# First attention: eight chunks a head made into rounded parts on GpSimd, values stored in class layout, maxima a chunk later, ada sums a step later

## Chip, cores and metric

One core of a Trainium2 chip. The metric is the device time in microseconds (us) of one execution. The kernel before takes 3302.08 us, the median of three runs (3301.21 to 3302.14).

## What is computed

Two transformer blocks on one sequence of 2048 tokens, width 1024, in f32. The change lies in the first block: its dilated attention, and two helpers of it. Shortened, for each of 12 heads of 64 dimensions:

```python
for window, dilation in ((128, 1), (512, 4), (2048, 16)):
    o_i, lse_i = dilated_window_attn(q, k, v, window, dilation)
mix_w = softmax(stack(lses))
o = sum(mix_w * outs)
attn_out = o * silu(g_attn)
```

The second block starts from `mod = silu(c) @ w_ada + b_ada`, a vector of 6144 numbers. The kernel makes it during the first block's projections.

## The kernel before, in words

**Stages.** `phase_a` makes the projections of the first block (0 to 754 us of the trace): first the values for 16 token tiles, then queries and keys with their rotation, then the gates and the convolution. `phase_b` is the first attention (754 to 1160 us). After it come the output projection, the second block and its experts. The order of the instructions is written out by hand under `tc.manual_schedule()`; each engine runs its own instructions in that order, and semaphores make it wait for the others. SP's queue issues nearly all DMAs, also in order. GpSimd (POOL) issues one DMA a head.

**Values.** `v_store` (L400) stores the values of token tile `t` to the scratch tensor `s_v`. A value row has 128 columns: 64 of a rounded high part and 64 of the rest. `load_v` (L756) loads one head's values as they lie (`v1`, 128 rows of 8 KB, one DMA); `turn_v` (L762) then makes the second arrangement `v2`, in which the rows go by class (token modulo 4 in groups of 32), by 16 GpSimd copies of 32x512 (L765).

**The head loop of `phase_b`.** `for h in range(H1)` runs over 12 heads. A loop has 20 chunks (`k`). In the loop of head `h`, PE computes the products of head `h` and the scores of head `h + 1`. A chunk does, in this order:

- `tpose` (L856): up to four 128x128 blocks of the exponentials are transposed by TensorE into a PSUM tile `pt` (three buffers);
- scores of the next head (`score`, L797, two matmuls; L798, a DVE operation that adds the mask and takes the minimum), 33 calls spread over chunks 0 to 13;
- exponentials (`expo`, L829, on ACT), one chunk ahead (`LA = 1`);
- `parts` (L859): the transposed chunk is copied from PSUM to SBUF. As *H*, ACT casts it to a rounded high part (L188) and DVE subtracts to get the rest (L189). As *A* or *V*, it is copied whole, in f32, by ACT or DVE (L865);
- `products(2)`: matmuls with the values (`mms`, L876) of the chunk two chunks back. A chunk in two parts takes two matmuls a piece; a whole chunk takes one f32 matmul, which the trace shows as two instructions.

In heads 0 to 10 the chunks go `HAHHAHHHHHAHVHVVHHVA`; head 11 has an order of its own. At the end of a group, `after1` copies a PSUM bank into `T` (one of four on DVE, three on ACT), and `after2` (L896, DVE) adds the classes.

**Maxima and sums.** The minima of the (negated) scores of the next head are joined over the arrangements by 16 small matmuls (`joint`, L818) at chunk 14 and by DVE (`joint2`, L824) at chunk 15; then the next head's first exponentials start. The sums of the exponentials of a head are rearranged by `total` (16 small GpSimd copies, L839) when the last exponential is issued. In chunk 2 of the next loop `total2` adds (L845), takes the reciprocal (L846), transposes on PE (L848), copies (L850) and stores. In chunk 6, `rest` issues GpSimd's DMA (L905), which adds half of `T` to `s_t` in DRAM after SP's store of `T`.

**Keys and queries.** `load_qk` loads head `h + 2` from SP's queue. GpSimd doubles the two keys (`repeat`, L661, 64x2048 each, chunks 7 and 8) and orders the query (`order`, L777, four of 128x512, chunks 10 to 13). The ordered query `q2` has two buffers. In head 10 GpSimd also makes the low halves of four tiles of `w_out` (`WO.split`, L681), in chunks 8, 9, 16 and 17.

**Ada.** `ada_step` runs once (three times twice) beside each of 34 projections in `phase_a`. A step ends the pair made before (`end`: two matmuls on PE, L290, then DVE adds and a store), rounds the next pair (`finish`: ACT, then DVE), sums one more block on DVE (L268, L270) and loads another.

The numbers of the profile's lines are those of this code:

Of the kernel before, what the change touches and what calls it, by code (L numbers as in the profile page):

```python
# [18 lines left out]
NT = 16  # L19
# [74 lines left out]
def prep(inp):  # L94
# [35 lines left out]
    "s_v": ([H1, 128, NT, 128], F32),  # L130
# [167 lines left out]
def phase_a(tc, A, K):  # L298
    nc = tc.nc
    ident, eps = K["ident"], K["eps"]  # L300
    with ExitStack() as es:
# [23 lines left out]
        with ExitStack() as e1:  # L325
# [74 lines left out]
            def v_store(t, vs):  # L400
                nc.sync.dma_start(A["s_v"][:, :, t].rearrange("h p d -> p h d"), vs.rearrange("p h a d -> p h (a d)").bitcast(F32))
# [184 lines left out]
        with tc.manual_schedule():  # L586
            last = None
            loads, sums = [], []
            na = 0

            def ada_step(more):
                nonlocal na
                ada.end()
                if sums:
                    ada.finish(*sums.pop(0))
                if len(loads) > 1 or loads and not more:
                    sums.append(ada.sums(*loads.pop(0)))
                if more and na < 32:
                    loads.append((na, ada.load(na)))
                    na += 1  # L600

            for _ in range(2):
                ada_step(True)
            bias = Bias(tc, A, ea)
            for i, j in enumerate(order):
                nxt = order[i + 1] if i + 1 < len(order) else None
                if i == 9:
                    while sums or loads or ada.late:
                        ada_step(na < 32)
                    ea.close()  # L610
                    K["qk"] = QK(tc, A, K)
                    K["qk"].load(0)
                for n in range(4):
                    p = proj(j, n)
                    if last:
                        done(*last)
                    last = j, n, p
                    if i < 9 and i * 4 + n > 1:
                        for _ in range(1 + (i in (2, 4, 6) and n == 0)):
                            ada_step(na < 32)  # L620
                        if i == n == 1:
                            bias.heads(ps)
                    if n == 1 and nxt and nxt not in W:
                        wsplit(nxt)
                        more = [x for x in order[i + 2:] if x not in W and x not in RAW]
                        if more:
                            wload(more[0])
            done(*last)


class QK:
# [10 lines left out]
    def open(self):  # L642
        self.add(1)
        with self.tc.using_default_side("right"):
            self.q2p = self.es.enter_context(self.tc.tile_pool(name="q2B", bufs=2, reuse_waits="tile"))
# [12 lines left out]
    def repeat(self, h, n, eng):  # L658

        t = self.T[h][n]  # L660
        eng.tensor_copy(t[64:], t[:64].bitcast(F32))  # L661
# [64 lines left out]
def phase_b(tc, A, K):  # L726
# [5 lines left out]
    with ExitStack() as es:  # L732
# [18 lines left out]
        m2 = cp.tile([128, 512], F32, name="m2")  # L751
        HD = {}
# [3 lines left out]
        def load_v(h):  # L756
            v1, v2 = (vv[h % 2].tile([128, KC, 256], F32R, name=n).rearrange("p a b -> p (a b)") for n in ("ph", "pl"))
            v1, v2 = v1.rearrange("p (t d) -> p t d", d=128), v2.rearrange("p (c a d) -> p c a d", c=4, d=128)
            nc.sync.dma_start(v1.bitcast(F32), A["s_v"][h])
            HD.setdefault(h, {}).update(v1=v1, v2=v2)  # L760

        def turn_v(h, i):  # L762

            d, (c, u) = HD[h], divmod(i, 4)
            nc.gpsimd.tensor_copy(d["v2"][QD[u], c], d["v1"][QD[c], u::4].bitcast(F32))  # L765
# [44 lines left out]
        WHOLE = [{k: {"A": nc.scalar.copy, "V": nc.vector.tensor_copy}[e] for k, e in enumerate(w) if e != "H"} for w in ("HAHHAHHHHHAHVHVVHHVA", "VVHAVHVVHHVHHHHHHHHH")]  # L810
# [20 lines left out]
        def total(h):  # L831
            d = HD[h]
            L = d["den"]
            E = st.tile([128, 4, 4], F32, name="E2", bufs=2)
            Lr = L.rearrange("p (g c a) -> p g c a", g=2, c=4)
            copy = (nc.gpsimd if h < H1 - 1 else nc.vector).tensor_copy
            for c in range(4):
                for u in range(4):
                    copy(E[QD[c], u, :], Lr[QD[u], 1, c, :])  # L839
            d["E2"] = E  # L840

        def total2(h):
            L, E = HD[h]["den"], HD[h]["E2"]
            r = st.tile([128, 16], F32, name="r", bufs=2)
            nc.vector.tensor_add(r.rearrange("p (a u) -> p u a", u=4), L[:, :16].rearrange("p (u a) -> p u a", u=4), E)  # L845
            nc.vector.reciprocal(r, r)  # L846
            p = ps_t.tile([128, 512], F32, name="pt")
            nc.tensor.transpose(p[:16, :128], r, ident)  # L848
            rt = st.tile([16, 128], F32, name="rt", bufs=1)
            nc.vector.tensor_copy(rt, p[:16, :128])  # L850
            nc.sync.dma_start(A["s_r"][h].rearrange("(t p) -> t p", p=128), rt)
# [7 lines left out]
        def parts(p, w, k, h):  # L859

            hi = pp.tile([128, 512], F32R, name="ph")
            W = WHOLE[h == H1 - 1]
            if k in W:
                whole = hi.bitcast(F32)
                W[k](whole[:, :w], p[:, :w])  # L865
                return whole,
            lo = pp.tile([128, 512], F32R, name="pl")
            split(nc, hi[:, :w], lo[:, :w], p[:, :w])
# [10 lines left out]
        def chunks(h, last_T):  # L879
# [11 lines left out]
            def after1(a):  # L891
                (nc.vector.tensor_copy if a == 1 else nc.scalar.copy)(T[:, a * 512:(a + 1) * 512], O.pop(a))
# [17 lines left out]
            V1, V2 = d["v1"], d["v2"]  # L910
            for a in range(4):
# [4 lines left out]
                            lambda pt, a=a, t0=t0: mms(bank(a), pt, [(V1[:, t0, :], 0, 0, 256), (V1[:, t0 + 1, :], 256, 128, 256)], True, False), None))  # L916
                bl = [on(t0 + 2), off(t0 + 3), on(t0 + 3)] + ([off(t0)] if a else [])
                td = [(V1[:, t0 + 2, :], 0, 256, 256), (V1[:, t0 + 3, :], 256, 384, 128)] + ([(V1[:, t0 - 1, :], 384, 0, 128)] if a else [])
# [20 lines left out]
        with tc.manual_schedule():  # L939
# [17 lines left out]
            for i in range(16):  # L957
                turn_v(0, i)
# [13 lines left out]
            LA, SC, JD = 1, 14, 1  # L972
            TV = {k: (2 * i, 2 * i + 1) for i, k in enumerate((4, 5, 9, 14, 15, 16, 17, 18))}
            L10, W10, W11 = (4, 13), (8, 9, 16, 17), (4, 6, 8, 10)
            wo_tile = lambda i: (QKs.q2p if i % 4 == 3 else QKs.P[i // 4]).tile([128, S], F32R, name=("q", "ka", "kb", "q2")[i % 4])
# [5 lines left out]
            for h in range(H1):  # L981
# [23 lines left out]
                for k, (_, bl, mm, aft) in enumerate(ch):  # L1005
                    if more and k == SC + JD:
# [8 lines left out]
                    while ne < min(need, 32):  # L1015
                        EX[ne]()
                        ne += 1
                        if ne == 32:
# [6 lines left out]
                    products(2)  # L1025
                    if k == SC and more:
                        joint(h + 1)
                    if k == 2 and h:
                        total2(h - 1)
                    if k == 6 and h:  # L1030
                        HD[h - 1].pop("rest")()
                    if h + 2 < H1:
                        if k in (7, 8):
                            QKs.repeat(h + 2, ("ka", "kb")[k - 7], nc.gpsimd)
                        if 10 <= k < 14:
                            order(h + 2, k - 10, nc.gpsimd)
                    if more:
                        for i in TV.get(k, ()):
                            turn_v(h + 1, i)
# [10 lines left out]
                    if not more:  # L1050
# [9 lines left out]
                        if k == 16:  # L1060
                            total2(h)
                            for e in range(2):
# [1506 lines left out]
```

## Time and profile before

| what | value |
|---|---|
| median of three runs | 3302.08 us |
| profiled execution, its own time | 3293.63 us |
| its span, first to last instruction | 3291.8 us |
| first attention in the span | 754 to 1160 us |
| one head of it, from one joint to the next (859.68 to 890.31) | 30.63 us |

The trace is of one execution. PE is TensorE's matmuls, PEld its weight loads, DVE VectorE, ACT ScalarE, POOL GpSimd. The time of a stretch is that of the engine that has no idle time in it; an engine with idle time can take more work as long as nobody waits for its result. Where a row gives start times, the time of a step on a busy engine is read from one start to the next, since a matmul's end is modelled and instructions overlap.

### The profile page before, as it was taken

The numbers are of one execution on the slowest core, as the hardware profiler recorded it, in microseconds if no ns is written. First come the engines' busy times: TensorE is split into PE (matmuls) and PEld (weight loads), VectorE is DVE, ScalarE is ACT, GpSimd is POOL, SyncE is SP. The second block draws the span as 40 slices with busy tenths as digits, with TensorE's granted clock in tenths as the row PEclk, the third lists the DMA queues.
The fourth block names the chain that finished last, engine by engine and source line by source line (L and its number), as shares of the span: only waits on it lengthen the run. The fifth ranks groups of instructions, "written<-read, shape, count | busy, mean of one in ns | idle before, by whom it ended". The sixth has DMA issues, their size and how long they took to land. (4 is left out here: it accounts for less than half of the span.)

```text
span 3291.8 us, 49939 instructions
## 1 busy us (share of the span) xinstructions
PE 3110.4 (94%) x19200; PEld 2766.1 (84%) x19200; DVE 2021.7 (61%) x4077; ACT 1437.4 (44%) x3072; POOL 675.4 (21%) x784
## 2 busy tenths in 40 slices
PE   9999999999999889789998999489999999999998
PEld 8988877888888767689986778389999999999997
DVE  5445557627888835547777476755565665565654
ACT  4322211105888723436657332244444444454443
POOL 0022210005566447311121010100110010010010
PEclk9999999999999999899999999789999999999999
DMA  5433357405555478544444765346666556665653
GB/s 167 138 132 122 117 184 233 142 20 143 148 126 142 117 218 232 140 132 154 146 139 153 235 187 175 129 180 212 211 211 213 205 205 212 211 217 206 208 203 102
DMA packets 200885, 556.83 MB, mean 169 GB/s; under 512 B 26512, under 2 KB 119580, under 8 KB 180294
## 3 DMA queue, kind: packets, MB, share of 16 engines
q1 hardware_dynamic: 186902, 499.73, 45.3%
q0 software_dynamic: 13456, 53.37, 7.0%
q8 instruction: 151, 2.47, 0.3%
q14 instruction: 88, 0.72, 0.1%
q10 hardware_dynamic: 288, 0.53, 0.0%
HBM read 425.29 MB, written 130.37 MB: 169 GB/s over the span
## 5 line engine op out<-in xcount | busy, mean ns | idle before, releaser
L2481 PE MATMUL mm<-xh,wh 128*128 128x256 f32 x2048 | 581.9, 284 | 0.2 <-ACT xh L188 0.2
L2481 PE MATMUL mm<-xl,wh 128*128 128x256 f32 x2048 | 580.7, 284 | 0.1
L2481 PE MATMUL mm<-xh,wl 128*128 128x256 f32 x2048 | 580.5, 283 | 0.0
L2475 DVE TENSOR_TENSOR wl<-raw,wh 128x1024 fp32r<-128x1024 f32 x380 | 453.8, 1222 | 177.0 <-ACT wh L2474 177.0
L2481 PEld LDWEIGHTS mm<-xh,wh 128*128 128x128 f32 x2048 | 394.2, 192 | 1.1 <-ACT xh L188 0.4
L2481 PEld LDWEIGHTS mm<-xl,wh 128*128 128x128 f32 x2048 | 394.1, 192 | 1.0 <-DVE xl L189 0.4
L2481 PEld LDWEIGHTS mm<-xh,wl 128*128 128x128 f32 x2048 | 394.1, 192 | 0.0
L2474 ACT CAST wh<-raw 128x1024 fp32r<-128x1024 f32 x384 | 390.1, 1049 | 0.0
L481 PE MATMUL mm<-hH,wl 128*128 128x512 f32 x832 | 325.2, 391 | 1.9 <-DVE wl L189 1.9
L481 PE MATMUL mm<-hH,wh 128*128 128x512 f32 x832 | 325.6, 391 | 0.0
L481 PE MATMUL mm<-hL,wh 128*128 128x512 f32 x832 | 325.4, 391 | 0.0
L2536 POOL DMA_INDIRECT out_dram<-yo,idx x32 | 63.1, 1973 | 750.7 <-DVE yo L2535 583.0
L829 ACT ACTIVATE s<-s,nm 128x256 f32<-128x256 f32 (+3 forms) x384 | 202.1, 531 | 19.5 <-DVE nm L824 19.5
L189 DVE TENSOR_TENSOR pl<-pt,ph 128x512 fp32r<-128x512 f32 (+1 forms) x269 | 176.6, 662 | 48.7 <-ACT ph L188 46.6
L2531 PE MATMUL y<-wh,hh 128*128 128x512 f32 x512 | 204.4, 399 | 0.0
L2531 PE MATMUL y<-wh,hl 128*128 128x512 f32 x512 | 200.1, 391 | 0.0
L2531 PE MATMUL y<-wl,hh 128*128 128x512 f32 x512 | 199.7, 390 | 0.0
L188 ACT CAST ph<-pt 128x512 fp32r<-128x512 f32 (+1 forms) x269 | 149.8, 562 | 110.4 <-PE pt L856 40.9
L481 PEld LDWEIGHTS mm<-hH,wl 128*128 128x128 f32 x832 | 157.2, 189 | 35.2 <-DVE wl L189 2.3
L481 PEld LDWEIGHTS mm<-hH,wh 128*128 128x128 f32 x832 | 157.1, 189 | 35.2 <-issue 1.7
L481 PEld LDWEIGHTS mm<-hL,wh 128*128 128x128 f32 x832 | 157.0, 189 | 32.2
L798 DVE CUSTOM_DVE_ANT_0 s<-ps,m 128x256 f32<-128x256 f32 (+3 forms) x384 | 156.9, 449 | 35.2 <-PE ps L797 33.8
(474 smaller groups left out, 6938.1 us busy)
## 6 DMA issues: line engine op xcount, KB each, us to landing
raw<-in_wg SPq DMA_DIRECT2D x32, 2048.0 KB
raw<-in_wd SPq DMA_DIRECT2D x32, 2048.0 KB
raw<-in_wu SPq DMA_DIRECT2D x31, 2048.0 KB
adaw<-in_wada SPq DMA_DIRECT2D x32, 768.0 KB
x<-in_x SPq DMA_DIRECT2D x32, 512.0 KB
wraw<-in_w1t SPq DMA_DIRECT2D x26, 512.0 KB
s_v<-vs SPq DMA_DIRECT2D x16, 768.0 KB
q<-s_q SPq DMA_DIRECT2D x12, 1024.0 KB
```

The costliest lines, as they stand in the source:

```text
L188: nc.scalar.copy(hi, src)
L189: (e or nc.vector).tensor_tensor(lo, src, hi.bitcast(F32), op=ALU.subtract)
L481: nc.tensor.matmul(p, a[:, k, :], b[:, k, tk], start=i == 0, stop=i == 3 * KC - 1)
L798: nc.vector.tensor_tensor_reduce(sv, p[:, :w], mask[:, mask.shape[1] - w:], 1.0, TOP, ALU.add, ALU.min, d["nm"][:, i:i + 1])
L829: nc.scalar.activation(sv, sv, AF.Exp, bias=d["nm"][:, i:i + 1], scale=-1.0, accum_out=d["den"][:, i:i + 1])
L2474: nc.scalar.copy(hi[:, c], RAW[i][:, c])
L2475: eng.tensor_tensor(lo[:, c], RAW[i][:, c], hi[:, c].bitcast(F32), op=ALU.subtract)
L2481: nc.tensor.matmul(p, a.rearrange("p (k f) -> p k f", k=KC)[:, k, w0:w0 + 128], b[:, k, :], start=i == 0, stop=i == 3 * KC - 1)
L2531: nc.tensor.matmul(ys[sl][:, cs], a[:, kk, sl * 128:sl * 128 + 128], b[:, k, cs], start=kk == 0 and j == 0, stop=kk == 7 and j == 2)
L2536: nc.gpsimd.indirect_dma_start(out=A["out"], out_offset=bass.IndirectOffsetOnAxis(ap=idx[:, sl:sl + 1], axis=0), in_=y, in_offset=None, co ...
```

## The change

- `parts`: in heads 0 to 10, eight chunks (1, 3, 5, 7, 10, 13, 16, 18) are made as *P*: ACT copies the chunk to an SBUF tile `pw` (four slots), GpSimd casts it to the high part and subtracts to get the rest. The other twelve are *H*. No chunk of these heads is whole any more. Head 11 stays as it was.
- `products(3)` in place of `products(2)`; `joint` at chunk 15 and `joint2` at chunk 16, in place of 14 and 15.
- `total` by 16 small PE matmuls into a `pt` tile at chunk 2 of the next loop; the add and the reciprocal at chunk 3; PE's transpose, the copy and the store at chunk 5. Head 11 stays as it was.
- `after1`: three of four on DVE, one on ACT.
- Values: `s_v` in class layout, each tile stored by four DMAs of 32 rows; a head's `v1` is loaded by four DMAs of 32 partitions in pieces of 2 KB, `v2` by a DMA of its own; `turn_v` is gone.
- `repeat` in eight pieces of 64x512, two each in chunks 6, 8, 9 and 11; `order` in chunks 12, 14, 15 and 17; `q2` has one buffer, and `pw` takes the space of the other.
- `ada_step` ends a pair one step later.

```diff
-                nc.sync.dma_start(A["s_v"][:, :, t].rearrange("h p d -> p h d"), vs.rearrange("p h a d -> p h (a d)").bitcast(F32))
+                a, u = divmod(t, 4)
+                for c in range(4):
+                    src = vs[c * 32:c * 32 + 32].rearrange("p h a d -> p h (a d)").bitcast(F32)
+                    nc.sync.dma_start(A["s_v"][:, u * 32:u * 32 + 32, c, a].rearrange("h p d -> p h d"), src)
...
-                ada.end()
+                if ada.late and aged:
+                    ada.end()
+                aged = bool(ada.late)
...
-            nc.sync.dma_start(v1.bitcast(F32), A["s_v"][h])
+            for c in range(4):
+                nc.sync.dma_start(v1[QD[c]].bitcast(F32), A["s_v"][h, :, c].rearrange("(u i) a d -> i u (a d)", u=4))
+            nc.sync.dma_start(v2.bitcast(F32), A["s_v"][h].rearrange("p c a d -> p (c a) d"))
...
-        WHOLE = [{k: {"A": nc.scalar.copy, "V": nc.vector.tensor_copy}[e] for k, e in enumerate(w) if e != "H"} for w in ("HAHHAHHHHHAHVHVVHHVA", "VVHAVHVVHHVHHHHHHHHH")]
+        PARTS = ("HPHPHPHPHHPHHPHHPHPH", "VVHAVHVVHHVHHHHHHHHH")
...
+            if h < H1 - 1:
+                d["E2"] = E = ps_t.tile([128, 512], F32, name="pt")[:, :16].rearrange("p (u a) -> p u a", u=4)
+                put = lambda o, u, x: nc.tensor.matmul(o, ident[:, QD[u]], x, start=True, stop=True, skip_group_check=True)
...
+            if how == "P":
+                whole = pw[:, k // 2 % 4, :w]
+                nc.scalar.copy(whole, p[:, :w])
+                nc.gpsimd.tensor_copy(hi[:, :w], whole)
+                nc.gpsimd.tensor_tensor(lo[:, :w], whole, hi.bitcast(F32)[:, :w], op=ALU.subtract)
...
-                (nc.vector.tensor_copy if a == 1 else nc.scalar.copy)(T[:, a * 512:(a + 1) * 512], O.pop(a))
+                (nc.scalar.copy if a == 1 else nc.vector.tensor_copy)(T[:, a * 512:(a + 1) * 512], O.pop(a))
...
-                    if more and k == SC + JD:
+                    if more and k == SC + 2:
...
-                    products(2)
-                    if k == SC and more:
+                    products(3)
+                    if k == SC + 1 and more:
                         joint(h + 1)
-                    if k == 2 and h:
-                        total2(h - 1)
+                    if h and k in (2, 3, 5):
+                        (total, total2, None, total3)[k - 2](h - 1)
...
-                        if k in (7, 8):
-                            QKs.repeat(h + 2, ("ka", "kb")[k - 7], nc.gpsimd)
-                        if 10 <= k < 14:
-                            order(h + 2, k - 10, nc.gpsimd)
-                    if more:
-                        for i in TV.get(k, ()):
-                            turn_v(h + 1, i)
+                        for i in range(KD.get(k, 8), KD.get(k, 8) + 2):
+                            if i < 8:
+                                QKs.repeat(h + 2, ("ka", "kb")[i // 4], nc.gpsimd, i % 4)
+                        if k in QO:
+                            order(h + 2, QO[k], nc.gpsimd)
```

## Rows read from the trace of the kernel before

**Rows 1.** The page's first part: busy time, share of the span, instructions

```profile
PE 3110.4 (94%) x19200; PEld 2766.1 (84%) x19200; DVE 2021.7 (61%) x4077; ACT 1437.4 (44%) x3072; POOL 675.4 (21%) x784
```

**Rows 2.** Windows: us; PE, PEld, DVE, ACT, POOL busy; clock; DMA share, GB/s

```profile
859.68:890.31 30.63, 29.31 (x239) 26.32 (x238) 26.09 (x91) 25.76 (x84) 19.33 (x39) 1.00 0.53 140
888.91:895.16 6.25, 6.25 (x69) 4.91 (x68) 5.20 (x15) 5.65 (x22) 3.95 (x10) 1.00 0.91 202
...
1074.55:1107.79 33.24, 29.85 (x239) 26.52 (x238) 28.52 (x93) 25.88 (x84) 15.74 (x22) 1.00 0.35 89
```

**Rows 3.** Waits of 750 to 1160 us: in total, times, longest

```profile
PE pt L848 <- DVE r L846: 18.0, 12, 3.3
```

**Rows 4.** Lines by form, 440 to 755 us, the ada matmuls: idle before, releaser

```profile
L290 PE MATMUL adap<-adal,adao 128*1 128x384 f32 x16 | 5.5, 341 | 0.9 <-DVE adal L189 0.9
L290 PE MATMUL adap<-adah,adao 128*1 128x384 f32 x16 | 5.4, 338 | 8.1 <-ACT adah L188 8.1
```

**Rows 5.** Timeline of PE, 868.9 to 878.9 us: start, duration, instruction

```profile
869.51 0.28 PE L876 MATMUL po<-pl,ph 128*128 128x256 f32 x1
871.11 0.27 PE L848 MATMUL pt<-ident,r 128*16 128x128 f32 x1 [1.32 <-DVE r L846]
...
874.05 0.28 PE L876 MATMUL po<-ph 128*128 128x256 f32 x1
...
874.52 0.60 PE L856 MATMUL pt<-ident,s 128*128 128x128 f32 x4
874.88 0.48 PE L797 MATMUL ps<-ka,q 128*128 128x512 f32 x1
...
877.82 1.03 PE L876 MATMUL po<-ph 128*128 128x256 f32 x4
878.68 0.49 PE L856 MATMUL pt<-ident,s 128*128 128x128 f32 x3
```

**Rows 6.** Timeline of PE, 888.9 to 895.3 us

```profile
890.31 0.44 PE L818 MATMUL ps<-nm,ident 128*32 128x8 f32 x32
890.68 0.65 PE L856 MATMUL pt<-ident,s 128*128 128x128 f32 x4
```

**Rows 7.** Timeline of ACT, 880.3 to 885.9 us

```profile
881.30 0.50 ACT L829 ACTIVATE s<-s,nm 128x256 f32<-128x256 f32 x1
...
881.80 0.57 ACT L188 CAST ph<-pt 128x512 fp32r<-128x512 f32 x1
882.26 0.62 ACT L829 ACTIVATE s<-s,nm 128x384 f32<-128x384 f32 x1
...
884.10 0.73 ACT L829 ACTIVATE s<-s,nm 128x512 f32<-128x512 f32 x1
...
884.82 0.36 ACT L865 COPY ph<-pt 128x256 f32<-128x256 f32 x1
885.08 0.41 ACT L829 ACTIVATE s<-s,nm 128x128 f32<-128x128 f32 x1
```

**Rows 8.** Lines by form of POOL, 750 to 1160 us: busy, mean ns

```profile
L765 POOL CAST pl<-ph 32x512 fp32r<-32x512 f32 x192 | 117.9, 614 | 64.4 <-DMA ph<-s_v 45.8 <-PE pt L848 6.5 <-PE po L876 3.2
...
L777 POOL CAST q<-q 128x512 fp32r<-128x512 f32 x46 | 26.7, 618 | 111.4 <-PE mm L481 109.8 <-DMA q<-s_q 0.9
...
L661 POOL CAST ka<-ka 64x2048 fp32r<-64x2048 f32 x11 | 20.8, 1892 | 13.0 <-DVE nm L798 12.5
...
L681 POOL TENSOR_TENSOR q<-T,q 128x1024 fp32r<-128x1024 f32 x2 | 4.8, 2392 | 9.9 <-DVE q L680 9.9
```

**Rows 9.** Waits of 160 to 180 us

```profile
PE mm L481 <- DVE wl L189: 1.9, 1, 1.9
```

**Rows 10.** DMA issues of 750 to 1160 us: KB each, us to landing

```profile
s_t<-T POOLq DMA_DIRECT2D x11, 512.0 KB, 5.1
```

**Rows 11.** Two DVE lines by source: ns min/median/max

```profile
L798 DVE CUSTOM_DVE_ANT_0 s<-ps,m x384: 278/420/693, 756.9 to 1107.0; 128x256 f32<-128x256 f32 x84, 128x128 f32<-128x128 f32 x60, 128x384 f32<-128x384 f32 x48
L500 DVE TENSOR_TENSOR t<-t,cos x24: 676/679/1787, 177.0 to 433.8; 128x512 f32<-128x512 f32 x24
```

## Prediction made before the run

> **What bounds the kernel now.** The page's first part comes first: PE is busy for 94% of the span [rows 1], so time is won where PE waits or does more than it must. The windows come next, over one head from joint to joint: 30.63 us, of which PE is busy 29.31, DVE 26.09, ACT 25.76 and GpSimd 19.33, at a granted clock of 1.00 [rows 2]. PE sets the pace, with 1.3 us of idle time a head. The waits say what that is: PE's transpose of `total2` waits for the reciprocal, 18.0 us in 12 times, the longest 3.3 [rows 3]. Last, PE's only other waits for a part of the change: its ada matmuls sit 8.1 us behind ACT's rounding and 0.9 behind DVE's [rows 4].
>
> **The change, part by part.**
>
> *The wait of `total2`.* Eleven of the 12 move: 18.0 - 3.3 (the longest, which I take for head 11's own, unchanged) = 14.7 us [rows 3]. In the timeline PE stops after 869.51 and goes on at 871.11 [rows 5]. Afterwards nothing of it waits within a chunk: add and reciprocal have from chunk 3 to chunk 5. **+14.7 us.** What is added are 16 small PE matmuls like the joint's, which take 890.31 to 890.68 = 0.37 us [rows 6], 11 times. **-4.1 us.** GpSimd's 16 small copies go; PE did not wait for them beyond the wait above.
>
> *Whole chunks become two rounded parts.* Two products of 256 columns cost PE 877.82 to 878.68 = 0.86 us whole, and 874.05 to 874.52 = 0.47 us in parts [rows 5]: 0.39 less for 512 columns. Of the eight whole chunks five have 512 columns of products (4, 12, 14, 15, 18), one 384 (1), two 256 (10, 19): 5 x 0.39 + 0.29 + 2 x 0.195 = 2.6 us a head, for heads 0 to 10. **+28.6 us.**
>
> *ACT.* A 512-column copy takes 0.46 us from start to start (881.80 to 882.26), one of 256 0.26 (884.82 to 885.08) [rows 7]; 384 lies between, 0.37. ACT gets the eight P copies (four of 512, one of 384, three of 256: 3.0 us), loses its four whole copies (one of 512, one of 384, two of 256: 1.35) and two of its three copies of `T` (0.9), and a cast is 0.2 longer: +0.95 on 25.76, so 26.7 us a head [rows 2]. PE by the terms above comes to 30.63 - 1.33 - 2.6 + 0.37 = 27.1. ACT and PE are then level, and it matters how the work lies in the head. In chunks 14 to 19 there are no scores. PE has four transposes of four blocks at 0.36 (874.52 to 874.88) and two of half that, 1.8; products of chunks 11 to 16, four of 0.47 and two of 0.24, 2.4; the joint's 0.37: 4.5 us [rows 5, 6]. ACT has eleven exponentials of this head and the next (two of 128 columns at 0.41, seven of 256 at 0.50, one of 384 at 0.62, one of 512 at 0.73) = 5.6, and casts of four times 0.46 and twice 0.26, 2.4: 8.0 us [rows 7]. Before, PE filled this stretch: 6.25 of 6.25 us [rows 2]. So ACT is 3.5 us late at its end. In chunks 0 to 2 it has only 2.3 us of work (three copies and two exponentials) against PE's 4.7 (0.37 for the sums, 1.2 of products, 1.0 of transposes, and scores of 2048 columns in two passes, 1.9, with their first loads), and three chunks may now be pending, so up to 2.4 us are caught up. The rest, 1.1, plus some 0.5 for hand-overs (a PSUM tile is free only after both engines read it), is 1.6 us of new PE waits a head. Bounds: 0, where chunks 3 and 4 absorb it too, and 3.5, where nothing is carried. I take 1.6, 11 times. **-17.6 us.**
>
> *DVE* loses four copies of 512 columns and gains two, so it falls below its 26.09 us [rows 2]; nothing.
>
> *GpSimd.* Off go 16 casts of 0.614 = 9.8 us a head [rows 8] and the small copies. On come eight casts and eight subtractions over 3200 columns. The nearest subtraction is that of `w_out`, 2.39 us for 1024 columns; a cast of 512 takes 0.618 [rows 8]: 7.5 + 3.9 = 11.4 us. The key copies (1.89 each) become eight pieces of at most 0.6 each (the casts of 512 columns), 4.8; with the order's 4 x 0.62 = 2.5 that is 18.7 us a head and the issue of a DMA, about the 19.33 of before [rows 2], of some 28. A 512-wide P needs 0.62 + 1.2 = 1.8 us on GpSimd and has three chunks, over 4 us. The cover is gone where something else stands in the queue. In head 10 there are four subtractions of 2.39 us [rows 8], two each ahead of chunk 10's and chunk 18's parts; head 10's loop has 33.24 us already [rows 2]. **-3.0 us** there (bounds 0 and 2 x 4.8).
>
> *Loads and stores of values.* One MB more a head: the DMA engines are busy 0.53 of 30.63 us for what they move now [rows 2], and 202 GB/s was moved at a share of 0.91, so a MB more is about 5 us of 28. The second arrangement's load waits on SP's queue for chunk 19's products; behind it stands the store of `T`, which waits for the same chunk. No load is late: all are for the next head. The stores of a value tile become four; PE is busy beside them, except at the last one, where PE waited 1.9 us for the next weights [rows 9] behind the last eviction. I add 1.2, about three issues more. **-1.2 us** (bounds 0 and 1.9).
>
> *Ada.* A step later the rounded pair is ready before PE comes: 8.1 + 0.9 = 9.0 us [rows 4]. ACT's next rounding now waits for PE's two matmuls, and SP's load of the next bias waits for the store just issued. The evictions stand behind that with four PSUM buffers as cover, so I take 1.0 off. **+8.0 us** (bounds 4 and 9).
>
> Copying `q2` into one buffer costs nothing: the scores that read it end in chunk 6, the new order starts in 12. `joint` a chunk later leaves ACT's first exponential of the next head at the same chunk.
>
> *Sum:* 14.7 - 4.1 + 28.6 - 17.6 - 3.0 - 1.2 + 8.0 = 25.4 us off. The terms are from the profiled execution, 3293.6 us, which lies 8.5 below the median of the runs; taken off the median, 3302.1 - 25.4 = **3276.7 us**. A measurement of this kernel can tell about 0.2%, 6.6 us, from no change.
>
> **The rivals.**
>
> *PE stays the bound* and ACT's late end is absorbed. For it: ACT has slack in chunks 7 to 13, 25.76 of 30.63 [rows 2]. Against: the late work lies where PE has least. Without the 17.6 us: 3259 us.
>
> *ACT becomes the bound* and carries nothing: 3.5 instead of 1.6 a head, 20.9 us more: 3297.6 us. For it: 8.0 against 4.5 us. Against: three pending chunks.
>
> *Slower: GpSimd's queue in chunk 6.* `rest` waits for SP's store of `T`, which now follows the 1 MB load; 1.5 MB at 202 GB/s is 7.4 us [rows 2]; GpSimd's own half MB took 5.1 us to land [rows 10]. The store is issued at the end of chunk 2, and `rest` comes up about 6 us later; behind it stand two key pieces and chunk 7's parts. Each us by which the store lands more than some 2 us after `rest` comes up is a us of PE a head. The gain is gone at 25.4 / 11 = 2.3 us a head, 4.3 us after; at 6 it is 1.7 x 11 = 18 us slower, 3320 us. Against: chunk 7's product comes only in chunk 10, and that is the slack of 2 us.
>
> *Slower: GpSimd slows DVE.* In the rotation stage a DVE product took 0.68 us, but 1.79 at most where GpSimd ran products beside it [rows 11]. If each of 12 subtractions a head met that once, 1.1 us each, DVE would have 26 + 13 = 39 us a head instead of 30.63: 11 x 8.5 = 94 us slower, 3396 us. Against: the score operation, which has one input in PSUM as DVE's subtractions here have, stayed between 278 and 693 ns over all heads, head 10 with its GpSimd subtractions included [rows 11]. The Trainium skill, SBUF — State Buffer, section Who interferes with whom, says that a DVE instruction with at most one SBUF input outside the two-port modes doesn't contend with GpSimd, and one with two does; both rows agree. The same skill's GPSIMD Engine Reference, section Engine selection, speaks against elementwise work with two inputs on GpSimd, as about twice as slow as VectorE; the rows of the subtraction above are what that costs here, and GpSimd has the time.
>
> **How the numbers follow.** Forecast 0.50; PE-bound 0.17; ACT-bound 0.16, half of it within 0.2%; GpSimd's queue 0.13, a little of it within; DVE slowed 0.04. Faster by over 0.2%: 0.50 + 0.17 + 0.08 = 0.75; within: 0.08 + 0.01 = 0.09; slower: 0.16. The range leaves out most of the slower cases above and goes to just below the PE-bound case: 3257 to 3302 us; the forecast's own, with its smaller bounds, is 3265 to 3290.
>
> **What would show it.** A head of about 28.8 us from joint to joint; no wait of PE for the reciprocal except head 11's; none for the ada rounding; ACT without idle time in chunks 14 to 19, and PE waiting there for `pt` or for parts; product steps of 0.47 where there were 0.86. The prediction is wrong if PE waits for GpSimd's parts in every head (chunk 7 above all), if DVE's steps grow longer, or if the granted clock falls below 1.00 in the loop, as it can only where PE stops.

## The result and the profile after

The forecast was 25 us faster, and the kernel became slower: 3323.5 us, the median of four runs (3319.2 to 3325.9), beside 3302.1 for the kernel before on the same chip. The ratio is 1.0062, 95% interval [1.0045, 1.008]. The profiled execution took 3319.2 us; its span is 3317.4 us, 25.6 more than before.

By stages (starts of the same matmuls in the two traces, us lost by the changed kernel; a minus is a gain):

| stage | predicted | measured |
|---|---|---|
| first to third projection (values' last stores) | 1.2 | 4.3 |
| projections with ada (54th to the last) | -8.0 | 6.5 |
| joint of head 0 to joint of head 1 | 0 | 6.4 |
| nine heads, joint 1 to joint 10 | -17.7 | -3.4 |
| joint 10 to the last product | -0.9 | 7.8 |
| the rest, and single tenths | 0 | 4.0 |

The head's terms, 14.7 - 4.1 + 28.6 - 17.6 = 21.6 us in eleven loops, stand here as nine loops and two, the latter with the 3.0 of head 10's queue. The rest is the same code in both kernels; it took 2131.6 to 2140.7 us in the profiles of this study, so its share is not the change's.

The page's first part and the windows of the changed kernel, the latter as in [rows 2] (PE, PEld, DVE, ACT, POOL busy; clock; DMA share, GB/s): the loop that ends in head 1's joint, a steady head, and the loop of head 10.

```profile
PE 3107.8 (94%) x19552; PEld 2773.5 (84%) x19552; DVE 2010.9 (61%) x4057; ACT 1443.1 (44%) x3092; POOL 670.7 (20%) x652
```

```profile
780.90:815.50 34.60, 26.44 (x209) 24.43 (x208) 21.57 (x83) 24.08 (x79) 21.59 (x29) 0.80 0.70 163
...
967.83:997.94 30.11, 28.56 (x275) 26.52 (x275) 24.81 (x89) 26.58 (x86) 20.73 (x31) 1.00 0.69 177
1088.20:1125.10 36.90, 31.00 (x271) 28.61 (x270) 27.39 (x91) 26.54 (x86) 19.27 (x22) 0.91 0.42 130
```

A head fell from 30.63 [rows 2] to 30.1 us, not to 28.8. PE now has 1.5 us without work in it, and its busy time fell only from 29.31 to 28.56. The DMA engines are busy 0.69 of the head where it was 0.53. The waits of 813 to 1050 us, some eight heads (in all, times, longest), say what took the place of the reciprocal:

```profile
PE ps L804 <- DVE nm L805: 7.9, 8, 1.0
...
PE pt L869 <- DVE pl L189: 4.2, 8, 0.5
...
PE po L895 <- POOL pl L885: 1.0, 1, 1.0
```

The first two are at the turn of the head. First PE's timeline there, then ACT's, then DVE's (start, duration, instruction, idle time before it):

```profile
972.03 0.66 PE L869 MATMUL pt<-ident,s 128*128 128x128 f32 x4 [0.53 <-DVE pl L189]
...
973.96 0.34 PE L804 MATMUL ps<-kb,q 128*128 128x384 f32 x1
975.28 0.50 PE L804 MATMUL ps<-ka,q 128*128 128x512 f32 x1 [0.99 <-DVE nm L805]
...
978.11 0.87 PE L845 MATMUL pt<-den,ident 128*32 128x4 f32 x32
978.91 0.66 PE L869 MATMUL pt<-ident,s 128*128 128x128 f32 x4
```

```profile
970.68 0.57 ACT L188 CAST ph<-pt 128x512 fp32r<-128x512 f32 x1
971.15 0.51 ACT L837 ACTIVATE s<-s,nm 128x256 f32<-128x256 f32 x1
...
973.11 0.51 ACT L837 ACTIVATE s<-s,nm 128x256 f32<-128x256 f32 x1
973.51 0.20 ACT L837 ACTIVATION_READ_ACCUMULATOR s<-s,nm 128x1 f32 x1
973.61 0.84 ACT L188 CAST ph<-pt 128x256 fp32r<-128x256 f32 x2
```

```profile
971.28 0.69 DVE L189 TENSOR_TENSOR pl<-pt,ph 128x512 fp32r<-128x512 f32 x1 [1.60 <-ACT ph L188]
974.00 0.42 DVE L189 TENSOR_TENSOR pl<-pt,ph 128x256 fp32r<-128x256 f32 x1 [2.03 <-ACT ph L188]
974.34 0.68 DVE L915 TENSOR_TENSOR T<-po,T 128x512 f32<-128x512 f32 x1
974.94 0.28 DVE L805 CUSTOM_DVE_ANT_0 s<-ps,m 128x128 f32<-128x128 f32 x1
```

ACT goes through the late chunks without a pause, so chunk 19's cast comes at 973.6. DVE has stood idle for it since 972.0 and subtracts at 974.0; only behind that and `after2` come the next head's scores in DVE's order, and PE's fourth score wants a PSUM tile that DVE has not read. ACT's lateness was foreseen; that DVE stands idle in line with it and passes it on to the scores was not. The 16 small matmuls of the sums take 978.11 to 978.91 = 0.80 us, where 0.37 was taken from the joint's [rows 6].

### The profile page after: what moved, and what is told of

Same layout as the page of the kernel before. It is cut to its first block, busy times and chain, and to the rows that moved or that the text cites. A ratio compares the mean times of both kernels' runs of the same rounds, so it can differ in the third digit from the quotient of the medians.

```text
span 3317.4 us, 50732 instructions
## 1 busy us (share of the span) xinstructions
PE 3107.8 (94%) x19552; PEld 2773.5 (84%) x19552; DVE 2010.9 (61%) x4057; ACT 1443.1 (44%) x3092; POOL 670.7 (20%) x652
```

## The experiments

They ran on other chips, on which the kernel before takes 3292 to 3294 us (medians of 9 to 17 runs); every ratio is to those. The changed kernel was not run again there, so its 1.0062, from the first chip, is compared with theirs across chips. "Joint to joint" and stage times are from each run's profiled execution; projections and joints are counted from 0 where they are named by number.

### The head: sums, parts, and who is late

**Sums in two steps alone**, on the kernel before (`total2` keeps the add and the reciprocal at chunk 2, `total3` the transpose at chunk 4):

```diff
-                    if k == 2 and h:
-                        total2(h - 1)
+                    if h and k in (2, 4):
+                        (total2, None, total3)[k - 2](h - 1)
```

> The kernel before with one thing changed: the add and the reciprocal of a head's sums stay at chunk 2 of the next loop, PE's transpose with its copy and store goes to chunk 4. Theory (the wait of PE for the reciprocal costs what its row says, and nothing else is late at that place): the 1.3 us of PE's wait a head goes away, a head from joint to joint falls from 30.6 to about 29.3 us, 11 x 1.3 = 14 us off the kernel before, ratio about 0.9956. Rival (ACT and DVE are the ones that are late at the turn of a head, and PE's stop gave them time): PE stops for a transposed chunk's parts or for a PSUM tile of the scores instead, a head stays above 30.2 us, and the ratio lies between 0.998 and 1.001.

Measured: 3277.9 us, ratio 0.9954 [0.9938, 0.9971], as the theory had it. Its windows, of one head and of the loop of head 10:

```profile
826.28:855.40 29.12, 29.12 (x239) 26.34 (x238) 25.81 (x91) 25.68 (x84) 19.33 (x39) 1.00 0.56 147
...
1059.26:1091.42 32.16, 29.66 (x240) 26.55 (x239) 28.23 (x93) 25.79 (x84) 15.73 (x22) 1.00 0.35 91
```

PE is busy for 29.12 of 29.12 us: nothing took the wait's place. The changed kernel's first term is thus real, and this head, a full microsecond shorter than the changed kernel's, is what its other parts are to be held against.

**Three late chunks by DVE**, on the changed kernel:

```diff
-        PARTS = ("HPHPHPHPHHPHHPHHPHPH", "VVHAVHVVHHVHHHHHHHHH")
+        PARTS = ("HPHPHPHPHHPHHPHDPDPD", "VVHAVHVVHHVHHHHHHHHH")
...
+            elif how == "D":
+                nc.vector.tensor_copy(hi[:, :w], p[:, :w])
+                nc.vector.tensor_tensor(lo[:, :w], p[:, :w], hi.bitcast(F32)[:, :w], op=ALU.subtract)
```

> The changed kernel, but in heads 0 to 10 both parts of chunks 15, 17 and 19 are made by DVE (cast, then subtraction), so ACT loses 0.46 + 0.46 + 0.26 = 1.2 us of casts in the last chunks of a head, and DVE does not wait for ACT there. PE's work is the same. Theory (ACT has no idle time from chunk 13 to the end of the head, DVE's subtraction of chunk 19 waits for ACT's cast, and the next head's scores stand behind it in DVE's order): PE's waits at the turn of a head, some 1.4 us, fall to under 0.5, a head falls from 30.1 to 29.1 us, 11 us off the changed kernel, ratio to the kernel before about 1.003. Rival (DVE itself, or the PSUM tiles, set the turn of the head): DVE's extra 1.3 us come on top, a head stays at 30.0 or grows, ratio 1.006 or more.

Measured: 3305.5 us, ratio 1.0045 [1.0027, 1.0062]; heads of 28.6 to 30.0, their mean over joints 1 to 10 29.4: between the theory's 29.1 and the rival's 30.0, as the ratio lies between theirs. Both waits at the turn are gone, which is what the theory was about. One is left in 813 to 1050 us, and it makes most of the difference between the shorter and the longer heads, which the windows show, each with GpSimd's timeline around `rest` (L927) below it:

```profile
842.42:871.06 28.64, 28.20 (x271) 26.46 (x271) 26.39 (x93) 25.35 (x83) 20.19 (x31) 1.00 0.71 186
871.06:901.03 29.97, 28.58 (x272) 26.59 (x271) 26.65 (x93) 25.35 (x83) 20.08 (x31) 1.00 0.68 174
```

```profile
PE po L898 <- POOL pl L885: 6.2, 13, 1.0
```

```profile
860.26 0.84 POOL L927 DMA_DIRECT2D s_t<-T  x1 [1.79 <-DVE nm L805]
...
890.31 0.83 POOL L927 DMA_DIRECT2D s_t<-T  x1 [3.21 <-DMA s_t<-T]
891.18 1.16 POOL L668 CAST ka<-ka 64x512 fp32r<-64x512 f32 x2
892.41 0.61 POOL L884 CAST ph<-pw 128x512 fp32r<-128x512 f32 x1
893.10 1.27 POOL L885 TENSOR_TENSOR pl<-pw,ph 128x512 fp32r<-128x512 f32 x1
```

In the head of 29.97 us `rest` waits 3.2 us for SP's store of `T` to land, the two key pieces and chunk 7's parts stand behind it, and PE waits 0.97 us for them at 894.42. That is the mechanism of the rival "GpSimd's queue in chunk 6", as its text describes it, at under 1 us a head. In the changed kernel it shows in one head of nine (31.9 us between joints 4 and 5, PE waiting 1.0); in the others PE comes late enough for it. So ACT and its link to DVE set the waits of the changed kernel's head, and GpSimd's queue comes next.

**Four chunks in parts without GpSimd**, on the kernel before with the sums in two steps:

```diff
-("HAHHAHHHHHAHVHVVHHVA", "VVHAVHVVHHVHHHHHHHHH")
+("HHHHHHHHHHHHVHVVHHVH", "VVHAVHVVHHVHHHHHHHHH")
```

> The kernel before with the sums in two steps, and chunks 1, 4, 10 and 19 of heads 0 to 10, which ACT copied whole, made as two rounded parts in the old way (ACT casts, DVE subtracts); GpSimd has no part in it. By the PE timeline with the sums in two steps, where PE has no idle time in a head of 29.1 us, chunk 1 in parts takes 0.40 in place of 0.70, chunk 4 0.47 for 0.86, chunks 10 and 19 0.23 for 0.43 each: 1.09 us a head. Theory (PE's steps shrink as the rows say, and what the change lost of them it lost in waits for parts and for PSUM tiles made by its own order): a head of about 28.1 us, 11 us off, ratio about 0.992. Rival (DVE, with 1.6 us more of subtractions in its order between the scores, comes late, and PE waits for parts or for a PSUM tile as in the changed kernel): a head of 28.8 or more, ratio 0.9945 or above.

Measured: 3277.2 us, ratio 0.9948 [0.9933, 0.9962], between the two and not told apart from the sums alone. The windows of a head and of the loop of head 10:

```profile
825.69:854.26 28.57, 28.38 (x239) 25.79 (x239) 27.00 (x95) 25.68 (x84) 19.41 (x39) 1.00 0.56 148
1055.35:1090.78 35.43, 31.38 (x240) 28.40 (x239) 30.11 (x98) 25.86 (x84) 17.33 (x29) 0.90 0.38 101
```

The head falls by 0.5 of the 1.09 us (28.6 to 29.0 in all heads), and DVE, at 27.0 us, is the late one: PE's only wait in 813 to 1050 us is for its score operation, 2.6 us in 8 times. In the loop of head 10, where DVE has w_out to split as well, the 3.3 us more take the gain back. So PE's steps in parts are shorter as the timeline had said, but an engine close to PE's own time gives half of it back in waits.

### The values

**The class layout of the values alone**, on the kernel before: stores, loads and `v1`/`v2` as in the change, `turn_v` gone.

> The kernel before with the values' class layout alone: tiles stored by four DMAs, a head's two arrangements loaded by five, no GpSimd copies of values. Theory: the last stores land later and the second projection starts 4 us later (7.6 us between the first two before, 12.0 in the changed kernel); head 1's query comes late at the start of the attention, 3 to 6 us; in the loop nothing changes, since PE did not wait for GpSimd's copies: 30.6 us a head. About 3311 us (3308 to 3314). Rival: the start of the attention is late only because ada shifted it or because GpSimd's parts were queued there; then only the 4 us show, 3306 us.

Measured: 3308.5 us, ratio 1.0048 [1.0032, 1.0065], near the theory. (The profile is of the slowest of its four executions, 3314.0 us.) The second projection, the ada stage (183.2 us between projections 53 and 82, 179.9 before) and the first loop, 39.6 us, all grew; heads stayed at 30.6.

**Four stores a tile, to the old places**, on the kernel before:

```diff
-                nc.sync.dma_start(A["s_v"][:, :, t].rearrange("h p d -> p h d"), ...
+                for c in range(4):
+                    src = vs[c * 32:c * 32 + 32].rearrange("p h a d -> p h (a d)").bitcast(F32)
+                    nc.sync.dma_start(A["s_v"][:, c * 32:c * 32 + 32, t].rearrange("h p d -> p h d"), src)
```

> The kernel before; only the store of a value tile is four DMAs of 32 rows in place of one of 128, to the same places as before. Loads, layout, attention and ada are those of before. Theory (it is the four DMAs and not the class layout that delay SP's queue at the second projection, where the weights of the next one stand behind the last stores): the first to the third projection take 16.5 us in place of 13.1, the time grows by 3 to 5 us, ratio 1.001 to 1.0015; the start of the attention stays 28.2 us from joint to joint. Rival (the layout or the loads cause it): 13.1 us between these projections and a ratio of 1.000.

Measured: 15.9 us from the first to the third projection (expected 16.5), ratio 1.003 [1.0019, 1.0041], twice what was expected. SP's timeline shows the mechanism; the first fence is the kernel before, the second this one (and the changed kernel issues the weights at 170.60):

```profile
158.56 6.90 SPq L401 DMA_DIRECT2D s_v<-vs  x2
...
168.24 3.80 SPq L317 DMA_DIRECT2D wraw<-in_w1t  x2
```

```profile
158.06 9.74 SPq L403 DMA_DIRECT2D s_v<-vs  x8
...
170.29 2.73 SPq L317 DMA_DIRECT2D wraw<-in_w1t  x2
```

The eight stores of the last two tiles keep SP's queue 9.7 us, the two of before 6.9, and the next weights are issued 2.1 us later (2.4 in the changed kernel). In the changed kernel PE then stops 3.6 us in place of 1.9 [rows 9], and its clock is at the lower level from the end of the stop on (granted clock 0.50 over 172 to 176 us, 0.81 over 176 to 183). The windows of the two projections, kernel before and changed kernel:

```profile
163.80:176.90 13.10, 11.21 (x50) 8.96 (x50) 2.00 (x6) 3.53 (x5) 1.26 (x1) 1.00 0.83 297
```

```profile
163.40:180.80 17.40, 13.79 (x50) 10.86 (x49) 2.78 (x7) 3.90 (x6) 1.29 (x1) 0.80 0.75 228
```

1.7 us of the 4.3 are the longer stop; PE's own work took 2.6 more at the lower clock. In the seven other profiles with four stores a tile the same stretch took 15.9 to 17.1 us. The rest of the 11 us by which this run's profile is longer than that of the kernel before lies in the ada stage (182.9 in place of 179.9 us, where PE's wait for the rounded pair grew from 8.1 to 11.8 us), in the loops of the first and last heads (2.4) and behind the attention (2.6). None of that code was touched; why it is longer is open.

**Keys before values**, on the changed kernel: `load_qk(1)` stands ahead of `load_v(0)`.

> The changed kernel with head 1's keys and query loaded ahead of head 0's values at the start of the first attention, nothing else. Theory (queue at the start): head 0's values now are 2 MB in five DMAs ahead of head 1's query, which arrives at 790.6 us; PE waits 7.1 us for its ordered copy and then runs some 8 us at a granted clock of 0.5. With the order turned round the first stretch from joint to joint falls from 34.6 us to 28 to 30 us: about 3317 us (3314 to 3320). Rival (bandwidth): all of these 4 MB are wanted at once, the values then come late for the first products, and the stretch stays above 33 us: 3322 to 3326 us.

Measured: 3306.2 us, ratio 1.0053 [1.0032, 1.0074]; the first loop 26.4 us. In the changed kernel the waits of that stretch were

```profile
PE ps L804 <- POOL q L784: 7.1, 1, 7.1
...
POOL q L784 <- DMA q<-s_q: 4.3, 1, 4.3
```

and the window with the keys first has neither the stop nor the lower clock (0.80 above):

```profile
780.50:806.90 26.40, 24.06 (x212) 22.16 (x212) 21.36 (x83) 23.90 (x79) 15.59 (x23) 1.00 0.88 222
```

So the 2 MB of head 0's values, which now pass SP's queue in five DMAs ahead of head 1's query, cost those 8 us: the three profiles with the keys first have 26.3 to 26.4 us here, the three profiles with the order of the changed kernel 34.0 to 35.4. By the runs' ratios the gain is smaller than by the profile, and its interval overlaps the changed kernel's.

### Ada

**The later end of a pair alone**, on the kernel before:

```diff
-                ada.end()
+                if ada.late and aged:
+                    ada.end()
+                aged = bool(ada.late)
```

> The kernel before with ada's pair ended a step later, nothing else. Theory (bias buffer): SP's waits for the bias rows rise to some 50 us in 14, PE's 9.0 us of waits for the rounded pair go, and new stops of 10 to 18 us come near 500 to 520 us: the projections end 2 to 9 us later than in the kernel before, about 3306 us (3302 to 3311). Rival (shifted start): the stops need the 4 us by which the projections start later in the changed kernel; then this one is 5 to 9 us faster than before, about 3295 us.

**Five bias buffers**, on the changed kernel (`name="adab", bufs=5`):

> The changed kernel with a fifth buffer for ada's bias rows, nothing else. Theory (bias buffer): since a pair ends a step later, the load of a new bias row takes the buffer of a row whose store was issued just before it, and SP's queue waits for that store to land (49.6 us in 14 waits in the changed kernel, 9.8 in 5 before); weights and gates are queued behind it, and PE stops near 500 to 526 us. Then five buffers bring these waits to about 10 us, PE's stops of 6.7, 6.2 and 2.8 us there go or shrink to 3, and the projections end 10 to 15 us earlier: about 3310 us (3306 to 3314). Rival (traffic): the loads there are late because of the 2 MB that GpSimd's DMA moves beside them and because the work lies otherwise in time; then the waits move to another load and the time stays within 4 us of 3323.

**Both, with the sums in two steps**, on the kernel before:

> The kernel before with the sums in two steps (alone: ratio 0.9954), and with the change's later end of an ada pair, this time with five buffers for the blocks of the bias and not four. Theory (what ate the gain of the later ada step was SP's queue, where the load of the next block's bias waits until the store that reads the old one has landed; a fifth buffer ends that wait): of the 9 us that the ada matmuls waited, some 5 come back; projections 53 to 82 take 175 us (before 179.9; the later step alone 180.3), ratio about 0.994. Rival (the weights of the next projection come late there whatever the buffers, since the sums of ada only move the stop elsewhere): 180 us and more, ratio 0.9954 or above.

Measured: the later end alone 1.0012 [1.0002, 1.0022]; the buffers in the changed kernel 1.0063 [1.0047, 1.008]; the three together 3274.1 us, 0.9945 [0.9924, 0.9966], where the sums alone gave 0.9954. Projections 53 to 82 took 180.3, 182.2 and 178.9 us (kernel before 179.9, changed kernel 186.4). SP's waits for a store of a bias show what the buffers are for (total, times, longest; kernel before, then the changed kernel):

```profile
SPq L257 <- DMA s_mod<-adab: 9.8, 5, 3.4
```

```profile
SPq L257 <- DMA s_mod<-adab: 49.6, 14, 8.9
```

With five buffers they fall to 13.1 us in 5 times. The stage fell with them: the changed kernel's ada code took 185.4 to 186.4 us in four profiles with four buffers, 182.2 here and 178.3 in the run with four repairs below with five. On the kernel before, the old ada code took 179.7 to 179.9 us in three profiles, the later end with five buffers 178.9 here and 176.1 in the last run below. So the same code differs by up to 4 us there, and the gain by the fifth buffer is of that size. The later end alone raised SP's waits to 55.1 us in 14, as its theory said, but the projections ended no later than before (753.0 and 753.7 us): neither of its two answers. PE's waits of 440 to 560 us in the changed kernel, then in the run with sums, later end and five buffers:

```profile
PE mm L485 <- DVE wl L189: 6.7, 1, 6.7
...
PE adap L290 <- ACT adah L188: 6.2, 1, 6.2
...
PE mm L1119 <- ACT g L551: 2.8, 1, 2.8
```

```profile
PE mm L481 <- DVE wl L189: 6.5, 1, 6.5
...
PE adap L290 <- ACT adah L188: 2.1, 1, 2.1
```

So the 9.0 us of [rows 4] became a stop for the weights of a projection, as the rival said. It stands in every profile with the later end, 5.8 to 8.1 us long, with four buffers and with five. The rival's time, 180 us and more for the stage, did not hold with five, and the theory's 175 was not reached. In the changed kernel's DVE timeline that stop reads

```profile
513.80 0.32 DVE L268 TENSOR_SCALAR adaacc<-adaw,adac 128x192 f32<-128x192 f32 x1 [3.55 <-DMA adaw<-in_wada]
514.15 3.14 DVE L270 SCALAR_TENSOR_TENSOR adaacc<-adaw,adac,adaacc 128x192 f32<-128x192 f32 x7
517.21 1.22 DVE L189 TENSOR_TENSOR wl<-wraw,wh 128x1024 fp32r<-128x1024 f32 x1
```

The split of the weights stands in DVE's order behind the sum of an ada block that has not landed. SP's timeline shows why the block is late:

```profile
489.51 4.70 SPq L295 DMA_DIRECT2D s_mod<-adab  x2
508.77 0.23 SPq L257 DMA_DIRECT2D adab<-in_bada  x1
...
509.39 0.35 SPq L251 DMA_DIRECT2D adaw<-in_wada  x1
```

The block's load was issued at 509.39, behind the load of a bias row for which SP had stood 8.9 us until the pair's stores landed. With five buffers one such wait is left ahead of the block (7.1 to 9.8 us), and DVE and PE wait as before. Whether the stop goes when this wait goes, no run tells. The Trainium skill, DMA: Bandwidth & Descriptors, section Anatomy of one DMA, gives about 2.0 us as a transfer's fixed cost on GpSimd's path and says that the delay to its semaphore can be surprisingly long when it writes to HBM. SP issued the stores here, so the figure is not theirs; on the delay the trace agrees: a store is 0.8 KB, and SP stood up to 8.9 us for one.

### The loop of head 10

**Keys first, and in head 10 chunks 10 and 18 by ACT and DVE**, on the changed kernel:

```diff
+            how = "H" if h == H1 - 2 and k in (10, 18) else PARTS[h == H1 - 1][k]
```

> The changed kernel with head 1's keys and query loaded ahead of head 0's values (ratio 1.0053 when that was run alone, loop of head 10 then 36.1 us), and in head 10 chunks 10 and 18 made by ACT and DVE and not by GpSimd, which there also subtracts for w_out. Theory (the parts of chunk 18 stand on GpSimd behind two subtractions of 2.4 us for w_out, and PE waits 3.8 us for them): the loop of head 10 falls from 36.1 to about 32.5 us, ratio about 1.0042. Rival (PE waits there for the rows of w_out that come late from memory, or ACT and DVE are late instead): the loop stays above 35 us, ratio 1.005.

**Four repairs at once**, the split of w_out later (`W10 = (10, 11, 18, 19)`) among them:

> The changed kernel with four repairs at once, each in a stage of its own: five bias buffers, head 1's keys and query loaded ahead of head 0's values, both parts of chunks 15, 17 and 19 by DVE, and in head 10 the splitting of w_out two chunks later (chunks 10, 11, 18 and 19 in place of 8, 9, 16 and 17). Theory (the losses are separate and add up): projections 53 to 82 about 182 us, first loop 26.4, heads 28.6 to 30.0, loop of head 10 32 to 33 (no wait of DVE for the rows of w_out, no wait of PE for chunk 18), ratio 1.000 to 1.001. Rival for the loop of head 10 (the rows of w_out come late from memory wherever they are split): 36 us or more there.

Measured: 3299.0 us, 1.0018 [1.0008, 1.0027], and 3287.5 us, 0.9986 [0.9975, 0.9996]. (The first one's profile is of its slowest execution, 3306.3 us.) In the changed kernel two waits make that stretch long:

```profile
DVE q L687 <- DMA T<-in_wo: 3.8, 1, 3.8
...
PE po L895 <- POOL ph L884: 4.1, 2, 3.8
```

The second is the price foreseen, GpSimd's chunk 18 behind two subtractions for w_out; it falls behind the joint, so the first of these runs lost it there (50.3 us from head 11's joint to the last product, 53.9 with the keys first alone), while joint to joint stayed long, 37.6 us: DVE waited 5.0 us for the rows of w_out with the scores behind it. Half of each answer was right. With w_out split two chunks later the loop took 33.5 us; PE's waits for DVE's scores there fell to 3.0 us (7.4 in the run before), and from joint 10 to the last product it took 85.2 us (91.3 in the changed kernel, 83.5 before). The four repairs add up to about what was expected: the first loop 26.4 us, the heads 28.8 to 30.6, ada 178.3 us, and a kernel just faster than the one before, still slower than the sums alone.

### What gained, put together

> The kernel before with what gained, put together: the sums in two steps (0.9954 alone), the later end of an ada pair with five bias buffers (0.9945 with the sums), chunks 1, 4, 10 and 19 in two parts by ACT and DVE in heads 0 to 9 alone (28.6 us a head in place of 29.1, but 35.4 in the loop of head 10 in place of 32.2 where it was done there too), and in head 10 the splitting of w_out two chunks later (33.5 us in the loop of head 10 in the changed kernel with its repairs, in place of 36.9). Theory (the stages add up): heads 1 to 9 at 28.6, 9 x 0.5 = 4.5 us below the kernel with the sums and ada, the loop of head 10 at 31 to 32; ratio 0.992 to 0.993. Rival (the loop of head 10 is set by DVE and by the rows of w_out, and takes back what the heads gain): 33 us or more there, ratio 0.9945.

Measured: 3272.7 us, ratio 0.9934 [0.9921, 0.9948], the fastest run of this study, by 0.0020 beyond the sums alone with overlapping intervals, and just above the 0.992 to 0.993 expected. A head and the loop of head 10:

```profile
824.00:852.60 28.60, 28.41 (x239) 25.80 (x238) 27.03 (x95) 25.72 (x84) 19.42 (x40) 1.00 0.56 149
1052.20:1082.20 30.00, 29.21 (x239) 26.30 (x238) 27.67 (x94) 26.11 (x85) 13.67 (x20) 1.00 0.35 90
```

The loop of head 10 lies below the 31 to 32 expected. No part of the values' layout and no GpSimd parts are in it.

## Why the prediction was wrong, step by step

Between the 25.4 us off that were forecast and the 25.6 us more in the profile lie 51 us: 14.5 in the ada stage, 14.3 in the nine heads, 8.7 behind joint 10, 6.4 in the first loop, 3.1 at the values' last stores, and 4.0 in code that is the same in both kernels. For a head, the steps from start to start of all of PE's instructions (859.68 to 890.31 us before, 967.79 to 997.91 in the changed kernel) say which terms failed:

| us a head on PE | predicted | measured |
|---|---|---|
| wait for the reciprocal | -1.3 | -1.3 |
| sums as matmuls | 0.4 | 0.8 |
| products of all chunks | -2.6 | -1.8 |
| scores | 0 | 0.5 |
| transposes | 0 | -0.2 |
| new waits | 1.6 | 1.5 |
| a head | -1.9 | -0.5 |

- **The wait of `total2`, +14.7: right.** Alone it gave 15 us (0.9954), and PE filled the head.
- **The sums as matmuls, -4.1: mis-sized.** 0.80 us each, 8.8 us in all. The joint's row was taken for the same kind; its 16 matmuls have 8 columns each, these 4, and yet took twice as long [rows 6]. They differ in order too: of the joint's, four in a row go to different quarters of the output, of these to the same one. Which of the two makes the difference no run tells.
- **Products in parts, +28.6: mis-sized, the term that failed in the head.** The 0.39 us of one chunk in mid-head [rows 5] was taken for all. Chunk 4 does fall so, from 0.86 to 0.48 us, but chunk 12 falls from 0.96 to 0.70 and chunk 19 from 0.43 to 0.33. The eight chunks' products fell from 6.0 to 3.8 us a head, and chunk 16, in parts before and after, rose from 0.32 to 0.79 at the turn, where PE goes on into the wait for `pt`. With 0.5 us more for the scores, PE's work fell by 0.75 us a head in place of 2.2. Why these steps are longer is not shown. Against 29.12 us for the sums alone the changed kernel's head has 30.1: its other parts lost a microsecond a head.
- **The ACT-late tail, -17.6: the size right, the mechanism half.** PE's new waits are 1.5 us a head, against 1.6. The 0.5 for `pt` were foreseen. The step that failed is the working of DVE as "nothing": DVE's busy time did fall (24.8 us), but its order puts the next head's scores behind a subtraction that waits for ACT, and that is the other 1.0, for `ps`. The rival "ACT becomes the bound" put 3.5 us on this wait; that its 3297.6 us lies nearer the result is luck.
- **GpSimd's queue in head 10, -3.0: right** for the wait it named, 3.8 us. The rows of w_out coming late to DVE, as much again, were not seen: that DMA waits 3.8 us where the kernel before waited 0.5.
- **Loads and stores of values, -1.2: a premise that failed.** "No load is late: all are for the next head" leaves out the first head, where head 0's values stand ahead of head 1's query: 6.4 us, part of it at half the clock. And three more issues a tile delayed the next weights by 2.4 us, which the lower clock made 4.3.
- **Ada, +8.0: wrong sign, the largest error.** The step that failed is "I take 1.0 off" for SP's wait for a store: SP's waits rose from 9.8 to 49.6 us, and behind them stood an ada block, which held up the weights, 6.7 us of PE's time. Nor was the pair always ready a step later: 6.2 of the 9.0 us stayed, in one wait. Of the 6.5 us lost in that stage some 3 came with four stores a tile and the ada of before (182.9 us). How much of the stop is the store's and how much the memory's stays open.
- **The rival on GpSimd's queue in chunk 6** gave 3320 us, close to the result, for another reason: its wait came once, under 1 us, and shows in full only when the turn of the head is repaired. The rival that GpSimd slows DVE is out: the score operation took 278/420/692 ns (min, median, max), as in [rows 11], with 88 subtractions of GpSimd beside it. That bears out the rule of the Trainium skill, SBUF — State Buffer, section Who interferes with whom.

## What to carry to other kernels

Remove one wait and run it alone before anything is built on it: here one small part, alone, gained 15 us, and the whole lost 21. A step's price read at one place of a loop is the price there; at the turn of the loop the same step cost more. When an engine is late, follow its work into the order of the engine that waits for it, and ask what stands behind that wait; the price is paid there. And count each queue at its ends, the first head and the last, not in the steady loop: a DMA that is early for head 5 may be the one that head 1 waits for.

## What was not expected of the hardware

- Around a stop of 3.6 us PE was at the lower of its two levels (granted clock 0.50 over 172 to 176 us, 0.81 over 176 to 183), which cost 2.6 us of slower matmuls; the 1.9 us stop of before left it at 1.00.
- Sixteen matmuls of 4 columns took 0.80 us, sixteen of 8 columns 0.37.
- A store of 0.8 KB held SP's queue for up to 8.9 us until it had landed, beside loads of 768 KB.
- GpSimd's subtraction of 512 columns took 1.29 us and DVE's 0.69, about twice, as the Trainium skill, GPSIMD Engine Reference, section Engine selection, has it for two inputs.
